# Row sums of a 64 MiB tensor: the first group in one load, and an earlier gate for the second load

## The chip, the cores and the metric

The kernel runs on one core of one Trainium2 chip. The metric is device microseconds (us) for one execution; lower is better.

## The reference

```python
def setup_inputs():
    batch, seq, dim = 32, 512, 1024
    return {"x": np.random.randn(batch, seq, dim).astype(np.float32)}

def reference(x):
    return np.sum(x, axis=-1).astype(np.float32)
```

The input has 16,384 rows of 1,024 float32 numbers, 67.11 MB (64 MiB). The output is one sum per row. There is next to no arithmetic per byte.

## The kernel before

A *group* is 128 partitions with 16 rows each: 8 MiB, 64 KiB per partition. There are eight groups. Seven are loaded whole (the first in two pieces here), and the last is cut into ever smaller pieces so that little work is left when the last byte lands. Three buffers of a group each take turns. SyncE (SP) issues all loads on one queue, VectorE (DVE) sums rows, and ScalarE (ACT) helps with the last rows only.

```python
    BIG = 16                      # rows of a group in a partition
    last = J // BIG - 1           # 7
    FIRST = 4
    ...
        def vec(dst, src):        # sums of several rows: one instruction
            return nc.vector.tensor_reduce(out=dst, in_=src, axis=..., op=add)

        def hold(inst, until, reason):      # inst waits for until
            tc.add_manual_dep(inst.ins, until.ins.name, ...)

        def rows(t, a, n, j, n_act, pairs=False):
            nv = n - n_act
            block = t[:, a * dim : (a + n) * dim].rearrange("p (n d) -> p n d", d=dim)
            load = nc.sync.dma_start(out=block, in_=rows_from(j, n))
            ...
                sums_of.append(vec(sums[:, j : j + nv], block[:, :nv, :]))
            for q in range(nv, n):
                act(sums[:, j + q : j + q + 1], block[:, q, :], dim)
            return load
    ...
        for g in range(last):
            t = inpool.tile([P, BIG * dim + 4], fp32)      # one of 3 buffers
            if g == 0:
                rows(t, 0, FIRST, 0, 0)                    # 2 MiB and its sums
                first = sums_of[-1]
                rows(t, FIRST, BIG - FIRST, FIRST, 0)      # 6 MiB and its sums
                continue
            load = rows(t, 0, BIG, g * BIG, BIG // 2 if g == last - 1 else 0)
            if g == 1:
                hold(load, first, "no descriptors of later loads while the first ones start")
        # ... the last group in pieces of 8, 5, 2 and 1 rows, and the stores
```

Two more facts matter. The very first load is moved to the entry of the program, ahead of the start-up handshake of the engines, so it is issued at time 0. And the second group's load is *gated*: it waits for the first four rows' sums, so that its descriptors are not made while the first load starts.

## Time and profile before

| | before |
|---|---|
| time, median of 6 runs | 162.12 us (161.94 to 162.47) |
| span in the profile | 160.9 us |
| read | 67.11 MB, 417 GB/s over the span |
| load queue busy | 97.6% |
| DVE / ACT busy | 75% / 11% |

The part of the page on DMA queues of the kernel before (packets, MB, share of 16 DMA engines' span; q1 is the load queue):

```profile
q1 hardware_dynamic: 2016, 67.12, 97.6%
...
HBM read 67.11 MB, written 0.07 MB: 417 GB/s over the span
```

There is no room in the queue: it is busy nearly all the time. The timeline of the kernel before shows the beat of it (start, duration, engine, line, operation, and in brackets how long the engine was idle before it and what ended that):

```profile
0.78 1.28 ACT L125 ACT_TABLE_LOAD   x1 [0.78 <-PEq L198]
7.12 4.42 DVE L98 TENSOR_REDUCE sums<-t 128x4 f32<-128x4096 f32 x1 [7.12 <-DMA t<-in_x_dram]
21.63 12.95 DVE L98 TENSOR_REDUCE sums<-t 128x12 f32<-128x12288 f32 x1 [10.09 <-DMA t<-in_x_dram]
41.26 17.22 DVE L98 TENSOR_REDUCE sums<-t 128x16 f32<-128x16384 f32 x1 [6.68 <-DMA t<-in_x_dram]
61.09 17.22 DVE L98 TENSOR_REDUCE sums<-t 128x16 f32<-128x16384 f32 x1 [2.61 <-DMA t<-in_x_dram]
```

Every sum starts when a load lands, and DVE is idle before each. So the start of a sum is the landing of its load, and the distance of two starts is the time that 8 MiB took: 19.83 us here, 19.33 us later in the same trace (8.389 MB in 19.33 us is 434 GB/s). The Trainium skill, page "DMA: Bandwidth & Descriptors", section "Where 436 GB/s comes from", gives 435.2 GB/s as the ceiling of the ports into SBUF; this trace agrees to 0.3%.

The start of the chain of waits of the kernel before (start, duration, what):

```profile
0.00 7.09 DMA t<-in_x_dram
7.09 0.02 issue
7.12 4.43 DVE sums L98
11.55 0.02 issue
11.56 29.68 DMA t<-in_x_dram
41.24 0.02 issue
```

The chain runs through the first four rows' sum, as if 4.43 us of DVE held up the second group. It is followed back through *issues*: the load was issued at 11.56 us because that sum had ended. But at 11.56 us the 6 MiB piece issued earlier was still streaming, until 21.6 us. The load was issued into a full queue, and its "29.68 us" are 10 us of standing in line and 19.6 us of transfer.

### The profile page before, as it was taken

The numbers are of one execution on the slowest core, as the hardware profiler recorded it, in microseconds if no ns is written. First come the engines' busy times: TensorE is split into PE (matmuls) and PEld (weight loads), VectorE is DVE, ScalarE is ACT, GpSimd is POOL, SyncE is SP. The second block draws the span as 40 slices with busy tenths as digits, with TensorE's granted clock in tenths as the row PEclk, the third lists the DMA queues.
The fourth block names the chain that finished last, engine by engine and source line by source line (L and its number), as shares of the span: only waits on it lengthen the run. The fifth ranks groups of instructions, "written<-read, shape, count | busy, mean of one in ns | idle before, by whom it ended". The sixth has DMA issues, their size and how long they took to land.

```text
span 160.9 us, 126 instructions
## 1 busy us (share of the span) xinstructions
DVE 120.1 (75%) x22; ACT 17.3 (11%) x31; POOL 0.2 (0%) x4
## 2 busy tenths in 40 slices
DVE  0280069950799958999499994999949999597943
ACT  3000000000000000000000000000000000596952
POOL 0000000000000000000000000000000000000000
DMA  7999996996996969969969969969969969999993
GB/s 265 452 477 501 391 521 261 521 521 261 521 521 261 521 261 521 521 261 521 521 261 521 521 261 521 521 261 521 521 261 521 521 261 521 391 391 424 407 406 82
DMA packets 2929, 67.18 MB, mean 418 GB/s; under 512 B 1265, under 2 KB 1393, under 8 KB 1521
## 3 DMA queue, kind: packets, MB, share of 16 engines
q1 hardware_dynamic: 2016, 67.12, 97.6%
q10 hardware_dynamic: 912, 0.06, 0.4%
q14 instruction: 1, 0.00, 0.0%
HBM read 67.11 MB, written 0.07 MB: 417 GB/s over the span
## 4 chain that ended last, share of the span: by engine, by line
DMA 73%; DVE 24%; SPq 1%; issue 0%; DVEq 0%
DMA t<-in_x_dram 73%; DVE sums L98 24%; SPq L137 1%; SPq L178 0%; DVE t L112 0%; DVEq L209 0%
## 5 line engine op out<-in xcount | busy, mean ns | idle before, releaser
L98 DVE TENSOR_REDUCE sums<-t 128x16 f32<-128x16384 f32 (+3 forms) x9 | 116.6, 12953 | 36.2 <-DMA t<-in_x_dram 36.2
L125 ACT ACTIVATE unread<-t 128x1024 f32<-128x1024 f32 x15 | 15.2, 1013 | 140.0 <-DMA t<-in_x_dram 140.0
L112 DVE CUSTOM_DVE_ANT_0 t<-t 128x512 f32<-128x512 f32 (+2 forms) x6 | 3.5, 601 | 2.4 <-DMA t<-in_x_dram 2.3
L125 ACT ACTIVATION_READ_ACCUMULATOR unread<-t 128x1 f32 x15 | 2.8, 188 | 0.0
L125 ACT ACT_TABLE_LOAD x1 | 1.3, 1283 | 0.8 <-PEq L198 0.8
L112 DVE DVE_READ_ACCUMULATOR2_ANT sums<- 128x1 f32 x5 | 0.4, 82 | 0.0
L198 POOL MEMSET const-bfloat16-1.0<- 128x1 bf16 x1 | 0.1, 102 | 0.0
L198 POOL MEMSET const-uint8-127<- 128x1 uint8 x1 | 0.1, 101 | 0.0
L198 POOL MEMSET const-float32-0.0<- 128x1 f32 x1 | 0.1, 99 | 0.2 <-issue 0.2
L198 POOL MEMSET const-float32-1.0<- 128x1 f32 x1 | 0.1, 98 | 0.0
L112 DVE DVE_READ_ACCUMULATOR2_ANT t<- 128x1 f32 x1 | 0.1, 82 | 0.0
L176 DVE MEMSET t<- 128x1 f32 x1 | 0.1, 59 | 0.0
## 6 DMA issues: line engine op xcount, KB each, us to landing
t<-in_x_dram SPq DMA_DIRECT2D x1, 6144.0 KB, 20.8
t<-in_x_dram SPq DMA_DIRECT2D x1, 4096.0 KB, 31.1
t<-in_x_dram SPq DMA_DIRECT2D x1, 2560.0 KB, 36.9
t<-in_x_dram SPq DMA_DIRECT2D x1, 2048.0 KB, 7.1
t<-in_x_dram SPq DMA_DIRECT2D x1, 1024.0 KB, 38.9
t<-in_x_dram SPq DMA_DIRECT2D x1, 280.0 KB, 39.2
t<-in_x_dram SPq DMA_DIRECT2D x1, 232.0 KB, 39.3
t<-in_x_dram SPq DMA_DIRECT2D x6, 41.2
```

Source lines behind the costliest of these rows:

```text
L98: return nc.vector.tensor_reduce(out=dst, in_=src, axis=mybir.AxisListType.X, op=mybir.AluOpType.add)
L112: return nc.vector.tensor_tensor_reduce(out=src[:, :n], in0=src[:, :n], in1=src[:, n:], scale=1.0, scalar=0.0, op0=mybir.AluOpType.add, op ...
L125: nc.scalar.activation(out=unread[:, :n], in_=src, func=mybir.ActivationFunctionType.Copy, accum_out=dst,)
L137: load = nc.sync.dma_start(out=block, in_=rows_from(j, n))
L176: nc.vector.memset(whole[:, width + 1 :], 0.0)
L198: nc = _bacc.Bacc("TRN2", target_bir_lowering=False, num_devices=1)
```

## The change

Its intent: one fewer load and one fewer sum, and the second group's load no longer waits for 7 us of loading and 4.4 us of summing. The gate stays, but as early as ScalarE ran anything in this program: after its table load, which ended at 2.06 us.

```diff
-    FIRST = 4
...
         for g in range(last):
             t = inpool.tile([P, BIG * dim + 4], fp32)
             if g == 0:
-                rows(t, 0, FIRST, 0, 0)
-                first = sums_of[-1]
-                rows(t, FIRST, BIG - FIRST, FIRST, 0)
-                continue
+                tiny = stpool.tile([P, 2], fp32)
+                nc.vector.memset(tiny[:, :1], 0.0)
+                first = nc.scalar.activation(
+                    out=tiny[:, 1:], in_=tiny[:, :1], func=mybir.ActivationFunctionType.Copy
+                )
             load = rows(t, 0, BIG, g * BIG, BIG // 2 if g == last - 1 else 0)
             if g == 1:
                 hold(load, first, "no descriptors of later loads while the first ones start")
```

## The prediction

> **What bounds the kernel now.** The input stream. The page shows 67.11 MB read in a span of 160.9 us, the load queue busy 97.6% of it, DVE 75%, ACT 11%. In the timeline the sums of full groups start at 41.26, 61.09, 80.61, 99.94 and 119.29 us, each when its load lands: 8 MiB per 19.3 to 19.8 us, 434 GB/s at best. The Trainium skill, "DMA: Bandwidth & Descriptors", section "Where 436 GB/s comes from", gives 435.2 GB/s as the ceiling of the ports into SBUF; this trace agrees, so only the ends of the stream can be shortened.
>
> The chain of waits shows DVE with 24%, among it the first four rows' sum (7.12 to 11.55 us), which releases the second group's load. I think that link is not real: when that load is issued at 11.56 us, the 6 MiB piece still streams until 21.6 us. The second group lands at 41.24, 19.6 us later: a full-rate load without a hole.
>
> **What the change does.**
> - Merges the pieces of 2 and 6 MiB into one load of 8. By the trace's packets, those of 16 KiB take 0.61 us each after the first ones, with holes of about 25 ns between; 48 KiB ones 1.815, 64 KiB ones 2.418. Eight of 16 plus eight of 48 KiB on each DMA engine are 19.40 us against 19.34, so packets save 0.06 us and the holes at most 0.2. Each engine's first packet takes 1.0 to 1.35 us instead of 0.61; that start cost of about 0.55 us stays, or shrinks by 0.1 or 0.2 as no second load's descriptors are made beside it.
> - Merges the sums of four rows (4.42 us) and twelve (12.95) into one of 17.22, from about 21.3 to 38.6 us; the old one ended at 34.6. That delays the fourth load's issue (34.61 to 38.6), but the second group lands only at 41 and the third at 61 us, so over 2 us of one load and a whole other are still queued. No cost.
> - Adds a one-element memset on DVE (59 ns in this trace) and a tiny ACT operation after the table load, which ends at 2.07 us. The skill's "ScalarE: Activation LUTs", section "What ACT_TABLE_LOAD costs", gives 186 ns plus 0.833 ns an element, so about 0.19 us (estimate; the trace's 1024-element ones, 1.01 us, agree), and a drain of 1.38 us after a table load, which this trace does not show. So loads two and three are issued at 2.3 to 3.7 us instead of 11.56, and their descriptors are made while the first load is young; at 11.6 to 12.4 us the trace shows holes of only about 30 ns from that.
>
> **On the critical path:** only the first group's landing: 21.62 becomes 21.2 to 21.5 us. Everything after shifts by that 0.1 to 0.4 us. The tail is untouched.
>
> **Prediction:** 161.9 us, 8 in 10 between 161.2 and 162.5. Chances: faster by over 2% 0.01, within 2% 0.98, slower 0.01.
>
> **Right if:** the second load is issued at 2.3 to 3.7 us; one sum of 17.2 us starts at 21.2 to 21.5 us; the fourth load is issued near 38.5; the intervals between later landings remain 19.3 to 19.8 us; from the last landing on, nothing differs.
>
> **Wrong if:** descriptors made at 2.3 us slow the first packets, so that the first group lands after 21.6 us; or the middle of the stream changes. Between 33 and 75 us the trace's 64 KiB packets take up to 2.68 us instead of 2.418, about 1 us in all, for a reason that I can't see; if that depends on how the DMA engines stand to each other, or is chance, it moves the time by up to 1 us either way.

## The result, and the profile after

| | before | after |
|---|---|---|
| time, median of 6 runs | 162.12 us (161.94 to 162.47) | 162.38 us (162.17 to 162.75) |
| second load issued | 11.56 us | 2.30 us |
| first group landed | 21.63 us | 21.85 us |
| second group landed | 41.26 us | 41.18 us |
| fourth load issued | 34.61 us | 39.10 us |
| span in the profile | 160.9 us | 160.4 us |

The ratio after to before is 1.0017, 95% interval [0.9998, 1.0035]: the same. Two later comparisons of the unaltered change, under "The experiments", gave 1.0009 and 0.9992. The plain mean of the three is 1.0006.

The two spans stand the other way round than the two medians: the profiled execution of before was slower than its six timed ones (162.69 us), and that of after was the fastest of its six (162.17 us). That alone says that one profiled execution of each must not be compared by its span; the reason is below. The load queue of the changed kernel was as full as before:

```profile
q1 hardware_dynamic: 1872, 67.12, 97.4%
...
HBM read 67.11 MB, written 0.07 MB: 419 GB/s over the span
```

The timeline of the changed kernel, same columns:

```profile
0.78 1.28 ACT L158 ACT_TABLE_LOAD   x1 [0.78 <-PEq L199]
0.85 0.06 DVE L157 MEMSET tiny<- 128x1 f32 x1 [0.85 <-PEq L199]
2.07 0.20 ACT L158 ACTIVATE tiny<-tiny 128x1 f32<-128x1 f32 x1
21.85 17.22 DVE L97 TENSOR_REDUCE sums<-t 128x16 f32<-128x16384 f32 x1 [20.94 <-DMA t<-in_x_dram]
41.18 17.22 DVE L97 TENSOR_REDUCE sums<-t 128x16 f32<-128x16384 f32 x1 [2.11 <-DMA t<-in_x_dram]
60.54 17.22 DVE L97 TENSOR_REDUCE sums<-t 128x16 f32<-128x16384 f32 x1 [2.13 <-DMA t<-in_x_dram]
```

And its chain of waits:

```profile
2.07 0.21 ACT tiny L158
2.28 0.02 issue
2.30 38.86 DMA t<-in_x_dram
41.16 0.02 issue
```

The gate opened 9.26 us earlier (11.56 to 2.30), and the "wait for the DMA" after it grew by 9.18 us (29.68 to 38.86). The second group landed at the same time. The load merely stood in line for longer. This is how a link of the chain looks that costs nothing: shorten it, and the wait behind it grows by the same amount.

Two things had not been expected. The first group landed later than before (21.85 against 21.63 us), not earlier, as predicted. And the beat of 41.26 to 61.09 us, 19.83 us in the profile of before, is 19.36 us in that of after.

### The profile page after: what moved, and what is told of

It is laid out like the page before. It is cut to its first block, busy times and chain, and to the rows that moved or that the text cites. A ratio compares the mean times of both kernels' runs of the same rounds, so it can differ in the third digit from the quotient of the medians. Undisturbed runs are those within 1.5% of the kernel's fastest.

```text
span 160.4 us, 126 instructions
## 1 busy us (share of the span) xinstructions
DVE 120.0 (75%) x22; ACT 17.5 (11%) x32; POOL 0.2 (0%) x4
## 4 chain that ended last, share of the span: by engine, by line
DMA 74%; DVE 22%; SPq 1%; ACT 1%; issue 0%; DVEq 0%
DMA t<-in_x_dram 74%; DVE sums L97 21%; ACT L158 1%; SPq L136 1%; SPq L179 0%; DVE t L111 0%; ACT tiny L158 0%; DVEq L210 0%
## 5 line engine op out<-in xcount | busy, mean ns | idle before, releaser
L97 DVE TENSOR_REDUCE sums<-t 128x16 f32<-128x16384 f32 (+2 forms) x8 | 116.4, 14553 | 34.7 <-DMA t<-in_x_dram 34.7
L158 ACT ACT_TABLE_LOAD x1 | 1.3, 1283 | 0.8 <-PEq L199 0.8
```

The lines of the kernel that those rows point to most:

```text
L97: return nc.vector.tensor_reduce(out=dst, in_=src, axis=mybir.AxisListType.X, op=mybir.AluOpType.add)
L158: first = nc.scalar.activation(out=tiny[:, 1:], in_=tiny[:, :1], func=mybir.ActivationFunctionType.Copy)
```

## The experiments

Four numbers per profile are used. The *landing* of the first group is the start of the first sum that needs all of it. The others are worked out from the records of the load queue's packets in the trace, which give each packet's start, duration and size, but not which of the 16 DMA engines carried it:

- *MiB by 5 us*: each packet's bytes spread evenly over its duration, summed up to 5 us from the span's start. It shows what the start of the stream costs.
- *mean and slowest end*: each load ends with 16 packets of 4 bytes, taken here as one for each of the 16 DMA engines, though the trace doesn't name the engine. The mean and the latest of the first group's 16 starts are given.
- *slow packets*: the time over 2.418 us, the usual duration of a 64 KiB packet, summed over those that start after 5 us, divided by 16.

All 14 profiles:

| kernel | first packets | second group's load issued, us | MiB by 5 us | mean end, us | slowest end, us | landing, us | slow packets, us | span, us |
|---|---|---|---|---|---|---|---|---|
| before | 16 KiB | 11.6 | 1.336 | 21.11 | 21.25 | 21.63 | 1.02 | 160.9 |
| before_again | 16 KiB | 11.7 | 1.336 | 21.12 | 21.39 | 21.75 | 0.12 | 160.1 |
| before_third | 16 KiB | 11.6 | 1.330 | 21.13 | 21.29 | 21.70 | 0.13 | 160.1 |
| split_early | 16 KiB | 2.3 | 1.324 | 21.14 | 21.36 | 21.80 | 0.16 | 160.2 |
| split1_early | 4 KiB | 2.3 | 1.322 | 21.52 | 21.86 | 22.22 | 0.15 | 160.6 |
| split2_early | 8 KiB | 2.3 | 1.380 | 21.00 | 21.51 | 21.91 | 0.16 | 160.4 |
| split8_early | 32 KiB | 2.3 | 1.347 | 21.15 | 21.35 | 21.72 | 0.82 | 160.9 |
| split8_again | 32 KiB | 2.3 | 1.318 | 21.17 | 21.39 | 21.84 | 0.35 | 160.8 |
| after | 64 KiB | 2.3 | 1.293 | 21.21 | 21.49 | 21.85 | 0.14 | 160.4 |
| after_again | 64 KiB | 2.3 | 1.293 | 21.21 | 21.66 | 22.04 | 0.62 | 160.9 |
| after_third | 64 KiB | 2.3 | 1.311 | 21.17 | 21.56 | 21.94 | 0.14 | 160.3 |
| one_late | 64 KiB | 11.8 | 1.321 | 21.15 | 21.54 | 21.91 | 0.40 | 160.7 |
| one_free | 64 KiB | 0.8 | 1.293 | 21.20 | 21.76 | 22.14 | 0.12 | 160.6 |
| one_starved | 64 KiB | 26.0 | 1.297 | 21.19 | 21.41 | 21.78 | 0.69 | 166.9 |

The table is not of one chip: the four later calls ran on four chips (one_late, split_early, one_free and after_again together; split2_early, split8_early, one_starved and before_again; split1_early, split8_again and before_third; after_third). (The third group's load follows 0.4 us behind the second's in all of them. In one_starved, 0.55 us of the slow packets is its second start.)

### Which half of the change, if any? Four kernels on one chip

My first theory, N, was that the descriptors of loads two and three, made at 2.3 to 3.1 us, hold up the first load. The rivals were P, that first packets of 64 KiB start worse than those of 16 KiB, and C, chance.

**one_late**: the changed kernel with its gate moved back to 11.8 us.

```diff
-                tiny = stpool.tile([P, 2], fp32)
-                nc.vector.memset(tiny[:, :1], 0.0)
-                first = nc.scalar.activation(out=tiny[:, 1:], in_=tiny[:, :1], func=Copy)
+                wide = stpool.tile([P, dim], fp32)
+                nc.vector.memset(wide, 0.0)
+                for _ in range(9):
+                    first = nc.scalar.activation(out=wide, in_=wide, func=Copy)
```

> The change with its gate moved: one 8 MiB load first, but the second load's issue waits for nine 1024-wide ScalarE copies in place of the tiny one, so about 11.5 us as before. In the changed kernel the first group landed at 21.85 us, not at 21.2 to 21.5 as predicted (before: 21.63). Theory N (neighbours): the descriptors of loads two and three, made at 2.3 to 3.1 us, hold the first load's packets up; then this kernel lands its first group at 21.3 to 21.5 us, its first packets take under 3.0 us, and its time is 0.3 us below the changed kernel's. Theory P (packet size): first packets of 64 KiB cost more at the start than those of 16 KiB; then the landing stays at 21.7 to 21.9 and the time equals the changed kernel's within 0.1 us. Theory C (chance): landings scatter by 0.3 us whatever the kernel.

Measured: landing 21.91 us, first packets up to 3.42 us, median 162.25 us, ratio to before 1.0007 [0.9985, 1.0029].

**split_early**: the old two pieces, with the new gate.

```diff
             if g == 0:
+                tiny = ...                                  # as in the change
+                first = nc.scalar.activation(...)           # as in the change
                 rows(t, 0, FIRST, 0, 0)
-                first = sums_of[-1]
                 rows(t, FIRST, BIG - FIRST, FIRST, 0)
```

> The other half: the first group stays in two pieces (4 and 12 rows, two sums), but the second load's issue waits for the tiny ScalarE operation, about 2.3 us, in place of the first rows' sum. Theory N: the first group lands later than before, 21.8 to 22.0 us against 21.63, and the time is 0.2 to 0.3 us above before. Theory P: it lands at 21.6 like before, and the time is within 0.1 us of before. Theory C: no order.

Measured: landing 21.80 us, median 162.08 us, ratio 1.0004 [0.9979, 1.0028].

**one_free**: the changed kernel without a gate.

```diff
-            if g == 1:
+            if False:
                 hold(load, first, ...)
```

> The changed kernel without any gate: loads two and three are issued right behind the first, at about 0.8 and 1.2 us. Theory N: the first group lands later still, 22.0 us or more, as their descriptors come while the first packets start; time 0.2 to 0.5 us above the changed kernel. Theory P: 21.8 to 21.9 us and the changed kernel's time within 0.1 us. Theory C: no order.

Measured: landing 22.14 us, median 162.25 us, ratio 1.0007 [0.9985, 1.0029].

**after_again**: the changed kernel, unaltered.

> The changed kernel once more, unaltered, beside the others: a second profile shows whether 21.85 us for the first group's landing is its own or chance (C), and five rounds whether 1.0017 of before is real. Expected 21.8 to 21.9 us under N and P, anything from 21.4 to 22.0 under C; ratio 1.000 to 1.003.

Measured: landing 22.04 us (a little over what I expected), median 162.31 us, ratio 1.0009 [0.9984, 1.0035].

What follows: N falls as an explanation of the time. With the gate moved from 2.3 to 11.8 us the landing was 21.91 us, between the two profiles of the unaltered change (21.85, 22.04), and the medians are 162.25 and 162.31. split_early landed at 21.80 us, just where N wanted it, but its time was not 0.2 to 0.3 us above before (162.08 against 162.05 us), and two later profiles of before landed at 21.70 and 21.75. one_free's landing is the latest of all, as N wanted, but its mean end (21.20 us) is that of the gated ones (21.21) and its time is one_late's. P is not refuted: the four one-piece profiles land at 21.85 to 22.14, the two split ones at 21.63 and 21.80. But C isn't either: the slowest of the 16 engines ended 0.14 to 0.56 us after their mean, so a landing is partly luck. None of these four ratios is clear of 1.

### Is the spread of the engines the cause? And is the gate off the path?

Theory S: large first packets put the engines out of step, each keeps its lag because each has a fixed share of a load, and the slowest decides every landing.

**split2_early** and **split8_early**: split_early with another first piece.

```diff
-    FIRST = 4
+    FIRST = 2        # split2_early; FIRST = 8 in split8_early
```

> As split_early (two pieces, tiny gate) with a first piece of 2 rows: the first packets are of 8 KiB. Theory S (spread): work is dealt out to the 16 DMA engines in equal fixed shares, so a group lands when its slowest engine is through; with large first packets the engines get out of step during the start and stay so. In the packets so far, the slowest engine ended its share of the first group 0.14 and 0.22 us after the mean of the 16 with 16 KiB first packets, and 0.29, 0.39, 0.44 and 0.57 us with 64 KiB. S expects 0.10 to 0.25 us here and the first group's landing at 21.5 to 21.8 us, time within 0.15 us of before. If it is chance (C), the spread here may be anything from 0.1 to 0.6.

Measured: the slowest engine 0.52 us after the mean, not 0.10 to 0.25; landing 21.91 us; median 162.10 us, ratio 0.9999 [0.9980, 1.0019].

> As split_early with a first piece of 8 rows, so first packets of 32 KiB. S expects the slowest engine 0.2 to 0.4 us behind the mean at the end of the first group, its landing between split_early's 21.80 and the one-piece kernels' 21.85 to 22.14 us. C: no order in size.

Measured: the slowest 0.20 us after the mean; landing 21.72 us, earlier than S expected; median 162.57 us, ratio 1.0025 [1.0005, 1.0045].

S falls: the smallest packets tried gave the wider spread.

**one_starved**: one_late with 22 copies in place of 9, so that the stream does run dry.

```diff
-                for _ in range(9):
+                for _ in range(22):
```

> The one-piece kernel with its gate at about 25.9 us (22 wide ScalarE copies), after the first load's data are through at 21.5 us. It tests my reading that the link of the chain from the first sums to the second load costs nothing because the stream is still full then. If so, this one, where the stream does run dry, must lose what the new start costs: a load on an idle queue lands 21.85 us after its issue, so the second group lands near 47.7 instead of 41.2 us and the time is 6.5 us more, 168.5 to 169.0 us. If the gate were already on the path at 2.3 and 11.8 us, those two would have differed by 9 us, and they did not (162.31, 162.25).

Measured: median 168.77 us, as expected, ratio 1.0410 [1.0390, 1.0431]. The timeline of one_starved:

```profile
2.06 23.90 ACT L159 ACTIVATE wide<-wide 128x1024 f32<-128x1024 f32 x22
21.78 17.22 DVE L97 TENSOR_REDUCE sums<-t 128x16 f32<-128x16384 f32 x1 [19.82 <-DMA t<-in_x_dram]
47.88 17.22 DVE L97 TENSOR_REDUCE sums<-t 128x16 f32<-128x16384 f32 x1 [8.88 <-DMA t<-in_x_dram]
```

For comparison the same rows of one_late:

```profile
2.06 9.76 ACT L159 ACTIVATE wide<-wide 128x1024 f32<-128x1024 f32 x9
21.91 17.22 DVE L97 TENSOR_REDUCE sums<-t 128x16 f32<-128x16384 f32 x1 [19.95 <-DMA t<-in_x_dram]
41.24 17.22 DVE L97 TENSOR_REDUCE sums<-t 128x16 f32<-128x16384 f32 x1 [2.10 <-DMA t<-in_x_dram]
```

This is the positive control. A gate at 2.3 or at 11.8 us made no difference to be seen, for the first load's data stream until about 21.5 us. A gate at 26 us costs 6.6 us in the landing of the second group, and the time rises by as much. The load issued on an idle queue at 25.98 us landed 21.90 us later, like the first one (21.78 us after its issue at 0); a load behind others lands 19.33 us after the one ahead of it. So the chain's link is shown to be off the path as long as the queue holds work, and the price of letting it run dry once was about 2.6 us (21.90 less 19.33) on top of the 4.2 us from the first landing to the late issue.

**before_again**: the kernel before, for a second profile.

> The kernel before, unaltered, for a second profile. Its first one lost 1.0 us to packets of 64 KiB that took up to 2.68 us between 33 and 75 us; split_early, with the same loads, lost next to none (0.1 us), and two of the one-piece kernels 0.3 and 0.4 us, late. If it is chance, this profile shows another amount at another place; if it belongs to the kernel before, again about 1 us at 30 to 75 us. First group's landing 21.6 to 21.8 us under S.

Measured: 161.91 us in its one execution. The timeline of before_again:

```profile
21.75 12.95 DVE L98 TENSOR_REDUCE sums<-t 128x12 f32<-128x12288 f32 x1 [10.06 <-DMA t<-in_x_dram]
41.11 17.22 DVE L98 TENSOR_REDUCE sums<-t 128x16 f32<-128x16384 f32 x1 [6.41 <-DMA t<-in_x_dram]
60.47 17.22 DVE L98 TENSOR_REDUCE sums<-t 128x16 f32<-128x16384 f32 x1 [2.13 <-DMA t<-in_x_dram]
```

The first profile of the same kernel had 41.26 and 61.09: 19.64 and 19.83 us between landings, here 19.36 and 19.36. So the slow packets of that profile belong to the execution, not to the kernel. They are why its span, 160.9 us, was 0.5 us above that of the changed kernel: 0.88 us more of slow packets, less a landing earlier by 0.22 us and an end of the program shorter by 0.19 us.

### What is left: repeats and one test of a small order

The mean ends of the first group seemed to rise with the size of the first packets (theory M). And split8_early had the only ratio of a competitive kernel that was clear of 1.

**split1_early**: split_early with `FIRST = 1`.

> As split_early with a first piece of one row, so first packets of 4 KiB. Theory S fell: 8 KiB first packets gave the widest spread of the split kernels (slowest engine 0.52 us after the mean), 32 KiB one of the narrowest (0.20). What the mean of the 16 engines' ends of the first group shows is a small order by the size of the first packets, theory M: 21.00 us with 8 KiB, 21.11, 21.12 and 21.14 with 16 KiB, 21.15 with 32 KiB, 21.15 to 21.21 with 64 KiB. M expects a mean end of 20.85 to 21.00 us here. The landing is that of the slowest engine, 0.1 to 0.6 us later by chance, so 21.2 to 21.8 us for the first sum that needs the whole group; the time within 0.2 us of before. If M is chance too, the mean end may be anything from 21.0 to 21.2.

Measured: mean end 21.52 us, a miss; landing 22.22 us; median 162.40 us, ratio 0.9995 [0.9978, 1.0013]. By 5 us it had moved 1.322 MiB, no more than those with 16 KiB, and its second piece, in packets of 60 KiB, went slowly at first (2.27 us at best, up to 2.61). M as an order over all sizes falls.

**split8_again**: split8_early, unaltered.

> The 8-row first piece unaltered, once more: its ratio of 1.0025 [1.0005, 1.0045] was the only one clear of 1. Its profile held 0.8 us of slow 64 KiB packets between 30 and 75 us, like the first profile of before and unlike the second one. If those are chance (C), the ratio here comes back to 1.000 to 1.002. If the kernel brings them on (theory L: engines that run nearly in step, first to last under 0.35 us at the end of the first group as in those two profiles, get into each other's way until they are spread), the ratio is again 1.002 to 1.004, and the profile shows either a range under 0.35 us with slow packets or a range over 0.4 us without. M expects a mean end of 21.12 to 21.17 us.

Measured: median 162.56 us, ratio 1.0002 [0.9984, 1.0021]; before had a median of 162.50 us, against 162.00 us earlier. So the 1.0025 did not come back, and the theory L of a kernel that brings slow packets on has no support in its ratio. In this profile 0.25 us of slow packets came at 110 to 140 us, next to none at 30 to 75.

**before_third**: the kernel before, a third profile.

> The kernel before for a third profile. Under L: a range of the 16 engines' ends of the first group under 0.35 us goes with 0.5 us or more of slow packets at 30 to 75 us, a range over 0.4 us with under 0.15 us. Under C no such order. M expects a mean end of 21.10 to 21.15 us.

Measured: first to last engine 0.39 us, which lies between the two ranges that I had named, so it is no test of L; slow packets 0.13 us; mean end 21.13 us.

L stays open. By the first group's ends it fits all 14 profiles: the two with a range under 0.35 us (before and split8_early) are the only ones with more than 0.11 us of slow packets at 30 to 75 us. Against it, in before's own profile the ends of the fifth to seventh groups were again 0.33 to 0.34 us apart, with 0.01 us of slow packets at most. Two profiles do not settle it.

**after_third**: the changed kernel a third time, on another chip, to test the one difference that was left.

> The changed kernel a third time, as a test of the one difference that is left. By the packets, the start costs a load queue that began with 16 KiB packets 1.77, 1.80, 1.77 and 1.78 us by 5 us into the span (before three times, split_early), and one that began with 64 KiB packets 1.80 to 1.87 (five profiles of one-piece kernels): about 0.07 us. If that holds, this profile shows 1.80 to 1.88 us. The one-row split had missed the order by packet size that I had read into the smaller sizes (mean end of the first group 21.52 us, not 20.85 to 21.00), so if this one shows under 1.79 the difference is chance as well. First group's landing 21.75 to 22.15 us; ratio to before 0.999 to 1.002, not clear of 1.

Measured: 1.311 MiB by 5 us, which is a start cost of 1.83 us (5 us less 1.311 MiB at 433.7 GB/s); landing 21.94 us; median 162.24 us, ratio 0.9992 [0.9978, 1.0005]. The expectation held. The six one-piece profiles have 1.293 to 1.321 MiB by 5 us, the four with 16 KiB first packets 1.324 to 1.336. The means are 1.301 and 1.332 MiB; the difference, 0.030 MiB, is 0.07 us at full rate. It is a weak finding: the nearest two of the two groups are 0.003 MiB apart, and split8_early and its unaltered repeat differ by 0.029 MiB.

No version tried beats both kernels. Leaving one_starved aside, no ratio to before is further than 0.25% from 1, and the median of before itself moved by 0.3% on another chip (162.00 to 162.50 us).

## Why the prediction was right, and where it was not

- **"The input stream" bounds the kernel: right.** In every profile, where no slow packets came, 8 MiB took 19.31 to 19.37 us, whatever was changed at the start.
- **"I think that link is not real": right, and shown.** The second load was issued 9.26 us earlier and the second group landed 0.08 us earlier in the profiles; one_late and one_starved show both sides of the edge.
- **"No cost" of the merged sum: right.** The fourth load was issued at 39.10 instead of 34.61 us (38.6 was predicted), and in the profile after all later landings of full groups are 19.33 to 19.36 us apart.
- **"Loads two and three are issued at 2.3 to 3.7 us": right,** at the early end. The drain of 1.38 us that the Trainium skill's page "ScalarE: Activation LUTs", section "What ACT_TABLE_LOAD costs", gives for every switch to a different table set did not come behind this program's only table load: it ended at 2.06 us and the tiny operation began at 2.07.
- **The time: within the range, but with the wrong sign of a small term.** I predicted 161.9 us, by 0.1 to 0.4 us saved; measured were 162.38 us and ratios of 1.0017, 1.0009 and 0.9992, which is no difference that these runs can tell from 0. That 162.38 lies within the range of 161.2 to 162.5 us is partly luck: before itself, unaltered, had medians up to 162.50 us later.
- **"From the last landing on, nothing differs": not so in the first pair of profiles.** From the landing of the last full group (the seventh) to the end were 22.27 us before and 22.46 after. after_third had 22.29, and all 14 profiles lie between 22.26 and 22.71 us, so it is taken for chance.

The step that failed is "On the critical path: only the first group's landing: 21.62 becomes 21.2 to 21.5 us". It landed at 21.85, 22.04 and 21.94 us. That is the "after 21.6 us" of "Wrong if", but not for the reason given there: with no descriptors of other loads made before 11.8 us, one_late landed at 21.91. Two terms of the sum were mis-sized, and one was missing:

1. *"The holes at most 0.2."* I had strung packets together by their times, and the trace doesn't tell which engine carried which, so a string that jumps to another engine's packet can show a hole that isn't there. Added up over all engines, the 16 KiB packets of the four kernels that start with them moved 426 to 432 GB/s between 3 and 6.4 us, against 434: 0.02 to 0.06 us in 3.4 us.
2. *"That start cost … stays, or shrinks by 0.1 or 0.2 as no second load's descriptors are made beside it."* It did not shrink; in the mean it was about 0.07 us larger. That goes with the one load of 64 KiB packets in six profiles of six, and not visibly with the gate: one_late had 1.321 MiB by 5 us, one_starved, with a still later gate, 1.297, and those gated at 2.3 us 1.293 to 1.311. Whether it is the packets' size, and why, was not found; 4 and 32 KiB do not fit a simple order.
3. *The lag of the slowest engine was not in the sum.* The prediction took its savings off before's landing, as if the lag in it stayed the same. A landing is the slowest engine's. In the 14 profiles the slowest ended 0.14 to 0.56 us after the mean, with no order over all sizes of the first packets (0.52 us with 8 KiB, 0.20 and 0.22 with 32 KiB), and the sum began 0.35 to 0.46 us after that. In before's first profile the lag happened to be the smallest of all, 0.14 us, so 21.63 us was a lucky landing to measure from; the next two profiles of before had 21.75 and 21.70. The lag was 0.20 us in the mean of the four profiles with 16 KiB first packets and 0.38 us in that of the six one-piece ones, which overlap (0.14 to 0.27, 0.22 to 0.56). So most of the 0.2 us between their mean landings (21.72 and 21.94 us) is lag; whether the one-piece load brings it on or chance does was not settled, and the times can't tell.

The warning under "Wrong if" was the useful part: slow packets in the middle of the stream do move the time, by up to 1 us here (1.02 us in one profile of before, 0.12 in the next), and hide such a term. A span is nearly the landing, plus the slow packets, plus a constant. With 138.25 us for the constant that is 21.63 + 1.02 + 138.25 = 160.9 for before, 21.75 + 0.12 + 138.25 = 160.1 for before_again, 22.04 + 0.62 + 138.25 = 160.9 for after_again, and within 0.35 us of the span in all other profiles but one_starved's, whose stream ran dry. What makes packets slow in some executions stays open.

## What to carry to other kernels

A chain of waits that runs through the issue of a transfer proves nothing while the queue ahead of it still holds data; ask what was in flight when it was issued, and expect the wait behind a shortened link to grow by what the link lost. With the stream saturated, an earlier issue, one load fewer and one instruction fewer were worth nothing that could be measured here. And before explaining 0.2%, profile the same unaltered kernel twice: here that moved the landing by 0.1 to 0.2 us and the span by 0.8.

## What the Trainium skill lacked or had wrong

- "DMA: Bandwidth & Descriptors", section "Where 436 GB/s comes from": one sentence says that for transfers between HBM and SBUF the HBM limit of about 358 GB/s binds. It does not hold for a core that streams as this one did: 434 GB/s from HBM for over 100 us (8 MiB per 19.33 us), within 0.3% of the port ceiling that the section also gives. The skill is not wrong throughout: the same section calls a measurement of 425 GB/s near fabric rate, and the one before it gives the 358 GB/s as the share when both cores of an HBM domain stream. What the chip's other cores did here was not recorded.
- The same page, section "Anatomy of one DMA — SWDGE (gpsimd) path": its fit of 2.0 us plus bytes over 436 GB/s, which is for the other path, would give 21.24 us for 8 MiB (an estimate from that page). The page has no such fit for this queue. Here, with the queue idle, 8 MiB took 21.78 to 22.14 us from issue to sum, so by the same sum the fixed part was 2.5 to 2.9 us. Behind another load it took 19.33 us, with next to no fixed part to be seen.
- The same page, section "Why a DMA increments its semaphore by 16 and not by 1", says that a transfer's DMA engines finish independently, but not how far apart: in the 14 profiles here, the first and the last engine's end of the first group were 0.32 to 0.88 us apart, and the landing is the last one's.
- "ScalarE: Activation LUTs", section "What ACT_TABLE_LOAD costs": the 1,283 ns of the table load agree exactly. The drain of about 1,380 ns, which the page adds for every switch to a different set, did not appear behind the program's only table load: the next operation began 0.01 us later. Whether it comes at a later switch no run here shows. The page's 187 ns for a one-element operation (186 + 0.833) were 203 ns.
- No page that I read tells of executions in which 64 KiB packets take up to 2.68 us instead of 2.418 for tens of microseconds (1.02 us in one profile of before, 0.12 and 0.13 us in two others).
